# Stationary columns of the feed-forward weights, two or eight elements apart in SBUF

## The chip, the cores and the metric

The kernel runs on one core of a Trainium2 chip. The metric is the time of one execution on the device, in microseconds (us). An execution is timed several times; the median stands for it. One more execution is recorded by the hardware profiler; its page and its trace are what is read below. The engines are named as the profile names them: PE is TensorE (matmuls), PEld its weight loads, DVE VectorE, ACT ScalarE, POOL GpSimd, SP the engine that issues most DMAs.

## The reference

A trunk of two layers works on 256 tokens of 2048 float32 values. Layer 0 is differential attention and a gated feed-forward part with a short causal convolution; layer 1 is a gated DeltaNet and a second such feed-forward part. Each part has a norm before it and is added to the residual stream. The change touches the feed-forward parts alone:

```python
def conv_ffn(h, w_up, conv_w, conv_b, w_down):
    u = causal_dwconv(h @ w_up, conv_w) + conv_b
    val, gate = jnp.split(u, 2, axis=-1)
    return (jax.nn.silu(gate) * val) @ w_down

def reference(x, ...):
    for i in range(DEPTH):
        h = rms_norm(x, mixer_norm[i])
        ...
        x = x + conv_ffn(rms_norm(x, ffn_norm[i]), ffn_w_up[i], ffn_conv_w[i], ffn_conv_b[i], ffn_w_down[i])
    return x
```

The up weights are 2048 x 11008 (5504 values and 5504 gates), the down weights 5504 x 2048, in each layer.

## The kernel before

**Layout.** Activations stand with features on the 128 partitions and the 256 tokens (`T`) along the free dimension; 2048 features are 16 row groups (`KD`), 5504 are 43 (`NJ`). The host lays every weight out in blocks of 256 output columns: `w[block]` has the shape 128 x row groups x 256, where the 256 columns are two column tiles of 128 (`c` = 0 and 1). In an up block, tile 0 holds 128 values and tile 1 the gates that belong to them; in a down block they are neighbours.

**Precision.** A product of float32 is made of three products of a rounded type (`fp32r`): high weight with high activation, low weight with high activation, high weight with low activation. `weights` (lines 81 to 91) loads a chunk of up to four row groups (`CK` = 4, 128 x 1024 elements, 512 KB) into a tile `raw` with one DMA of the SP queue, casts it on ACT into `whi` (line 89) and lets DVE subtract that from `raw` into `wlo` (line 90). Of each of the three there are four buffers, so a chunk's DMA waits until an earlier chunk has been used.

**Products.** `dense` (lines 132 to 156) goes through the chunks of a block. For each row group `k` and column tile `c` it issues two matmuls, here called a pair. Line 151 has a 128x128 piece of `whi` as the stationary operand and 512 moving columns (256 tokens of the high and 256 of the low activation); line 152 has the same piece of `wlo` and 256 moving columns (the high activation). Each matmul is preceded by a load of its stationary operand (LDWEIGHTS in the profile, engine PEld). In the last chunk of a block the two tiles go one after the other, in the others they alternate. `finish` (158 to 167) does the last chunk of the last down block of layer 1, so that each tile's output can be sent off when it is done.

**The order in which columns are read.** Before the change, the stationary operand is `hi[:, k, s]`, 128 elements side by side in each partition. The moving operand goes through `turns` (169 to 171): token `j` of the first 128, token `j` of the second 128, then `j + 1` of each, so that neighbouring reads are 128 elements apart. `halves` (173 to 175) puts the output back in order when it is read from PSUM. The token products `dense_tok` (207 to 224) have the activations as the stationary operand and read the weights as the moving one in the same manner, 256 elements apart.

**The feed-forward part.** `ffn` (364 onwards) runs 43 up blocks, each with 16 row groups. After each block DVE and ACT merge the parts, scale, convolve, and write a gated activation `ac` in its high and low part. Then `project` runs 8 down blocks with 43 row groups each, ten chunks of four and one of three; `add_out` adds them to `x`.

**Order.** The program is straight-line code; each engine runs its instructions in the order in which they are issued, with waits on semaphores for the data of the others. Small work of the attention and DeltaNet parts is spread between the products by generators (`spawn`, `tick`).

Of the kernel before, what the change touches and what calls it, by code (L numbers as in the profile page):

```python
# [16 lines left out]
P = 128  # L17
T = 256
D = 2048
KD = D // P  # L20
EPS = 1e-6
CK = 4
# [4 lines left out]
class Trunk:  # L27
# [101 lines left out]
    def banks(self):  # L129
        return self.dps.tile([P, 2, 2 * T], F32, tag="ps", name="ps")  # L130

    def dense(self, w, kt, acts, tiles=2, wide=True, each=None, apart=False):


        nc = self.nc
        ps = None if each or apart else self.banks()
        bank = [ps[:, c] if ps else self.mp() for c in range(tiles)]
        n = 2 * T if wide else T
        for k0, nk in self.chunks(kt, CK):
            hi, lo = self.weights(w[:, k0:k0 + nk, :])  # L140
            steps = [(k, c) for k in range(nk) for c in range(tiles)]
            if k0 + nk == kt:
                if each:
                    self.finish(bank, hi, lo, k0, nk, acts, each)
                    continue
                steps = [(k, c) for c in range(tiles) for k in range(nk)]
            for k, c in steps:
                a = acts(k0 + k)
                first, last = k0 + k == 0, k0 + k == kt - 1
                s = slice(c * P, (c + 1) * P)  # L150
                nc.tensor.matmul(bank[c][:, :n], hi[:, k, s], self.turns(a[:, :n // T, :]), start=first, stop=False)  # L151
                nc.tensor.matmul(bank[c][:, :T], lo[:, k, s], self.turns(a[:, :1, :]), start=False, stop=last and wide)  # L152
                if not wide:
                    nc.tensor.matmul(bank[c][:, :T], hi[:, k, s], self.turns(a[:, 1:, :]), start=False, stop=last)  # L154
            self.tick()
        return bank if apart else ps

    def finish(self, bank, hi, lo, k0, nk, acts, each):

        nc = self.nc  # L160
        for c in range(2):
            s = slice(c * P, (c + 1) * P)
            for k in range(nk):
                a = self.turns(acts(k0 + k))
                nc.tensor.matmul(bank[c], hi[:, k, s], a, start=False, stop=False)
                nc.tensor.matmul(bank[c][:, :T], lo[:, k, s], self.turns(acts(k0 + k)[:, :1, :]), start=False, stop=k == nk - 1)
            each(c, bank[c].unsqueeze(1))

    def turns(self, a):
# [162 lines left out]
    def pairs(self, a):  # L332

        return a.rearrange("p c t -> p t c") if len(a.shape) == 3 else a.rearrange("p (c t) -> p t c", c=2)
# [15 lines left out]
                done(2 * blk + c)  # L350
            self.add_squares()

    def project(self, w, kt, acts, done, final=False):

        n = KD // 2
        for b in range(n - final):
            self.add_out(b, self.dense(w[b], kt, acts), done)
        if final:
            def each(c, ps):
                self.add_x(KD - 2 + c, 1, ps)  # L360
                done(KD - 2 + c)

            self.dense(w[n - 1], kt, acts, each=each)

    def ffn(self, w_up, w_down, nj, cols_ap, done, final=False):

        nc = self.nc
        self.spawn(self.norm_stat())
        with self.tc.tile_pool(name="fp", bufs=1) as fp:
            cols = fp.tile([P, 8 * nj + 64], F32, tag="fcols", name="fcols")[:, :8 * nj]  # L370
            cols = cols.rearrange("p (t h j) -> p t h j", t=4, h=2)
            nc.scalar.dma_start(cols, cols_ap)
            acts = []
            rows = self.rows(fp.tile([P, nj * 2 * T], F32R, tag="ac", name="ac"), nj)
            for j in range(nj):
                ps = self.dense(w_up[j], KD, self.h_acts)
                c = []
                u = fp.tile([P, 2, T], F32, tag="u", name="u", bufs=2)
                self.merge(ps, u, fp)
                for half in range(2):  # L380
                    o = fp.tile([P, T], F32, tag=f"cv{half}", name="cv", bufs=2)
                    c4 = [cols[:, t, half, j:j + 1] for t in range(4)]
                    self.conv(o, u[:, half, :], c4[:3], c4[3])
                    c.append(o)
                nc.scalar.activation(c[1], c[1], AF.Silu)
                a = c[0]
                nc.vector.tensor_tensor(a, c[0], c[1], ALU.mult)
                ac = rows[j]
                self.split(ac, a)
                acts.append(ac)  # L390
            self.project(w_down, nj, lambda k: acts[k], done, final)

    def attention(self, w_first, w_qk, w_v, w_o, nh, dist_ap, ident_ap, qg, kg, lvec, sub, start, done, lambda_init):

# [531 lines left out]

NH = 8
NJ = 43
NQ = 16
NB, HB = 4, 4  # L930
NV = 2 * NQ

# [6 lines left out]
def _layout(inputs):  # L939
# [3 lines left out]
    x = {k: np.asarray(v) for k, v in inputs.items()}  # L943
# [9 lines left out]
    def blocks(w, kt, starts):  # L953
        w = w.reshape(kt, P, -1)
        return np.stack([np.concatenate([w[:, :, a:a + n] for a, n in s], 2) for s in starts]).transpose(0, 2, 1, 3)

    def pairs(n):
        return [[(T * i, T)] for i in range(n)]

    kd, vd, ff = NQ * P, NV * P, NJ * P  # L960
    wi = x["gdn_w_in"][0]
# [4 lines left out]
    go = x["gdn_w_out"][0].reshape(NB, 2 * HB, P, D // T, T).transpose(0, 3, 2, 1, 4)  # L966
    up = [[(j * P, P), (ff + j * P, P)] for j in range(NJ)]
    q, k = np.arange(P)[:, None], np.arange(T)[None]
# [15 lines left out]
    def turned(w):  # L984
        return w.reshape(*w.shape[:-1], T, 2).swapaxes(-1, -2).reshape(w.shape)

    out = {
        "x": np.concatenate([col[0][:, :KD], x["x"][0].T.reshape(KD, P, T).transpose(1, 0, 2).reshape(P, KD * T)], 1),
        "cols": np.concatenate(col, 1),
# [5 lines left out]
        "dist": np.concatenate(dist, 1),  # L995
        "fcols0": fcols[0],
        "fcols1": fcols[1],
        "w_up0": blocks(x["ffn_w_up"][0], KD, up),
        "w_down0": blocks(x["ffn_w_down"][0], NJ, pairs(D // T)),
        "w_gate": np.pad(wi[:, 2 * kd + 2 * vd:], ((0, 0), (0, P - 2 * NV))).reshape(KD, P, P).transpose(1, 0, 2),  # L1000
        "w_in": blocks(wi, KD, gin),
        "w_z": turned(blocks(wi, KD, gz)),
        "w_out": go.reshape(NB * (D // T), P, 2 * HB, T),
        "gate": np.broadcast_to(np.stack([x["gdn_A_log"][0], x["gdn_dt_bias"][0]]), (P, 2, NV)),
        "const": np.concatenate(const, 1).astype(f),
        "w_up1": blocks(x["ffn_w_up"][1], KD, up),
        "w_down1": blocks(x["ffn_w_down"][1], NJ, pairs(D // T)),
    }
    return {k: np.ascontiguousarray(v) for k, v in out.items()}

# [1 line left out]
def trunk_kernel(tc, a, out):  # L1012
    nc = tc.nc
    with ExitStack() as ctx:
        t = Trunk(ctx, tc)
        n = a["cols"].shape[1]
        cols = t.cp.tile([P, n], F32, tag="cols", name="cols")
        parts = t.chunks(KD, 2)

        def load():  # L1020
            if parts:
                k, n = parts.pop(0)
                s = slice(KD + k * T if k else 0, KD + (k + n) * T)
                nc.sync.dma_start(t.gx[:, s], a["x"][:, s])

        load()
        pos = [0]

        warm = t.mp()
        for _ in range(WARM):  # L1030
            nc.tensor.matmul(warm, t.onesr, t.onesr.unsqueeze(1).to_broadcast([P, 4, P]), start=True, stop=True)

        def take(n):
            pos[0] += n
            return cols[:, pos[0] - n:pos[0]]

        def one(c, i):
            return c[:, i:i + 1]

        mixer, ffn = take(2 * KD), take(2 * KD)  # L1040
        qg, kg, lvec, sub, ng = take(1), take(1), take(4), take(2), take(1)
        gconv = take(4 * 4 * NQ)
        def then(gain, layer):
            return lambda k: t.norm_tile(k, one(gain, layer * KD + k))

        starts = [k for k, _ in parts]
        begun = []

        def start(k):

            if len(begun) <= k:
                if k and k in starts:
                    load()
                if k == KD - 1:
                    with tc.issue_after(t.loaded.ins):
                        nc.sync.dma_start(cols, a["cols"])
                then(t.gx[:, :KD], 0)(k)
                begun.append(k)
            return t.h[k]

        t.attention(a["w_first"], a["w_qk"], a["w_v"], a["w_o"], NH, a["dist"], a["const"][:, :P], qg, kg, lvec, sub, start, then(ffn, 0),
                    0.8 - 0.6 * math.exp(-0.3 * 0))
        t.ffn(a["w_up0"], a["w_down0"], NJ, a["fcols0"], then(mixer, 1))
        t.gdn(a["w_gate"], a["w_in"], a["w_z"], a["w_out"], NB, HB, a["gate"], a["const"],
              lambda tap, tile_: one(gconv, tap * 4 * NQ + tile_), ng, then(ffn, 1))
        t.ffn(a["w_up1"], a["w_down1"], NJ, a["fcols1"],
              lambda k: nc.sync.dma_start(out[:, k, :], t.x[:, k, :]), final=True)


# [13 lines left out]
```

## Time and profile before

| what | value |
|---|---|
| time, median of 3 runs | 2531.76 us (2530.8 to 2531.91) |
| span of the profiled execution | 2530.1 us |
| PE busy | 2520.0 us, 16151 matmuls |
| PEld busy | 2309.7 us, 16151 loads |
| DVE busy | 1908.3 us |
| ACT busy | 1513.2 us |
| HBM read | 482.32 MB, 191 GB/s over the span |

The profiled execution is one of its own; its span goes from the first to the last instruction and is 1.7 us shorter than the median time, which has some launch and end around it. Busy times of different engines overlap, so they don't add up to the span. The duration of a matmul or of a load in a record includes its latency; since matmuls are pipelined, the pace is read from the starts, or from how many there are in a stretch, and not from the durations.

### The profile page before, as it was taken

What the parts mean: (1) busy time and instruction counts of PE and PEld (TensorE: products, weight loads), DVE (VectorE), ACT (ScalarE), POOL (GpSimd) and SP (SyncE); (2) the same over time, 40 slices, a digit from 0 to 9 for tenths busy, and PEclk for the clock granted to TensorE, in tenths of its full rate; (3) what the DMA queues carried; (4) which work ended last, traced back from release to release, by engine and by line L of the source; (5) the groups of instructions that cost most, each with busy time, mean ns of one, the idle gap of its engine ahead of it and who ended that gap; (6) DMA issues with size and microseconds to landing.
All of it is one profiled execution on the core that took longest, in us unless ns stands there. A gap on an engine that the chain in (4) does not pass through costs nothing.

```text
span 2530.1 us, 41598 instructions
## 1 busy us (share of the span) xinstructions
PE 2520.0 (100%) x16151; PEld 2309.7 (91%) x16151; DVE 1908.3 (75%) x2847; ACT 1513.2 (60%) x2098; POOL 103.5 (4%) x197
## 2 busy tenths in 40 slices
PE   9999999999999999999999999999999999999999
PEld 8998899999999999998989989989999999999998
DVE  8886677777777555689788788788887777776544
ACT  7766656666666444485774675675566666665343
POOL 0000000000000000012021021021000000000000
PEclk9999999999999999999999999999999999999999
DMA  7555566666666666666455565555566666666775
GB/s 256 175 184 175 167 203 201 202 202 201 200 201 202 200 200 202 202 187 201 154 185 180 170 188 184 168 175 184 165 201 201 201 201 202 201 201 205 209 207 157
DMA packets 138199, 487.20 MB, mean 193 GB/s; under 512 B 15472, under 2 KB 18448, under 8 KB 138000
## 3 DMA queue, kind: packets, MB, share of 16 engines
q1 hardware_dynamic: 137712, 484.17, 60.8%
q8 instruction: 127, 2.08, 0.3%
q14 instruction: 72, 0.59, 0.1%
q10 hardware_dynamic: 288, 0.35, 0.0%
HBM read 482.32 MB, written 2.15 MB: 191 GB/s over the span
## 4 chain that ended last, share of the span: by engine, by line
PE 95%; ACT 3%; DVE 1%; issue 1%; DMA 0%; SPq 0%; ACTq 0%; DVEq 0%
PE ps L151 51%; PE ps L152 26%; PE ps L221 3%; PE ps L220 3%; PE ps L222 3%; PE mp L773 2%; PE mp L151 1%; PE ps L154 1%; ACT whi L89 1%; PE mp L329 1%; PE mp L152 0%; ACT L593 0%; ACT lt L631 0%; PE ps L123 0%; ACT L297 0%
## 5 line engine op out<-in xcount | busy, mean ns | idle before, releaser
L90 DVE TENSOR_TENSOR wlo<-raw,whi 128x1024 fp32r<-128x1024 f32 (+2 forms) x911 | 1104.1, 1213 | 506.1 <-ACT whi L89 498.2
L89 ACT CAST whi<-raw 128x1024 fp32r<-128x1024 f32 (+2 forms) x911 | 944.2, 1038 | 822.9 <-PE ps L151 657.0
L151 PE MATMUL ps<-h,whi 128*128 128x512 f32 (+1 forms) x4208 | 1369.4, 375 | 0.0
L152 PE MATMUL ps<-h,wlo 128*128 128x256 f32 x4208 | 1151.1, 274 | 1.0 <-DVE wlo L90 1.0
L151 PEld LDWEIGHTS ps<-h,whi 128*128 128x128 f32 x4208 | 796.1, 189 | 102.8
L152 PEld LDWEIGHTS ps<-h,wlo 128*128 128x128 f32 x4208 | 807.7, 192 | 2.8 <-DVE wlo L90 1.3
L151 PE MATMUL ps<-ac,whi 128*128 128x512 f32 x1546 | 506.8, 382 | 0.0
L152 PE MATMUL ps<-ac,wlo 128*128 128x256 f32 x1546 | 421.2, 273 | 0.0
L151 PEld LDWEIGHTS ps<-ac,whi 128*128 128x128 f32 x1546 | 292.1, 189 | 40.8 <-PE ps L151 0.2
L152 PEld LDWEIGHTS ps<-ac,wlo 128*128 128x128 f32 x1546 | 296.8, 192 | 0.1
L151 PE MATMUL ps<-oc,whi 128*128 128x512 f32 x512 | 170.7, 384 | 0.0
L220 PE MATMUL ps<-whi,h 128*128 128x512 f32 x384 | 146.5, 382 | 0.0
L221 PE MATMUL ps<-wlo,h 128*128 128x512 f32 x384 | 146.1, 380 | 0.0
L222 PE MATMUL ps<-whi,h 128*128 128x512 f32 x384 | 145.7, 379 | 0.0
L310 DVE SCALAR_TENSOR_TENSOR cv<-u,fcols,cv 128x255 f32<-128x255 f32 (+1 forms) x344 | 142.9, 477 | 0.0
L152 PE MATMUL ps<-oc,wlo 128*128 128x256 f32 x512 | 142.0, 277 | 0.0
L151 PEld LDWEIGHTS ps<-oc,whi 128*128 128x128 f32 x512 | 96.9, 189 | 12.5
L152 PEld LDWEIGHTS ps<-oc,wlo 128*128 128x128 f32 x512 | 98.3, 192 | 0.5
L308 ACT ACTIVATE cv<-u,fcols 128x256 f32<-128x256 f32 x172 | 93.9, 593 | 0.5 <-DVE u L205 0.5
L343 DVE TENSOR_TENSOR x<-ps,x 128x512 f32<-128x512 f32 x110 | 75.6, 687 | 12.5 <-PE ps L152 11.2
L310 DVE SCALAR_TENSOR_TENSOR cv<-u,cols,cv 128x255 f32<-128x255 f32 (+2 forms) x192 | 84.0, 486 | 0.3
L221 PEld LDWEIGHTS ps<-wlo,h 128*128 128x128 f32 x384 | 72.6, 189 | 10.0 <-DVE wlo L90 0.2
(220 smaller groups left out, 2077.3 us busy)
## 6 DMA issues: line engine op xcount, KB each, us to landing
raw<-w_up SPq DMA_DIRECT2D x344, 512.0 KB, 4.7
raw<-w_down SPq DMA_DIRECT2D x160, 512.0 KB, 3.8
raw<-w_in SPq DMA_DIRECT2D x128, 512.0 KB, 4.7
raw<-w_z SPq DMA_DIRECT2D x64, 512.0 KB, 3.7
raw<-w_out SPq DMA_DIRECT2D x64, 512.0 KB, 4.2
raw<-w_qk SPq DMA_DIRECT2D x56, 512.0 KB, 4.5
raw<-w_v SPq DMA_DIRECT2D x32, 512.0 KB, 3.5
raw<-w_o SPq DMA_DIRECT2D x32, 512.0 KB, 4.7
```

What stands on the lines that cost most here:

```text
L89: self.cast = nc.scalar.copy(hi[:, :, s], raw[:, :, s])
L90: nc.vector.tensor_tensor(lo[:, :, s], raw[:, :, s], hi[:, :, s].bitcast(F32), ALU.subtract)
L151: nc.tensor.matmul(bank[c][:, :n], hi[:, k, s], self.turns(a[:, :n // T, :]), start=first, stop=False)
L152: nc.tensor.matmul(bank[c][:, :T], lo[:, k, s], self.turns(a[:, :1, :]), start=False, stop=last and wide)
L154: nc.tensor.matmul(bank[c][:, :T], hi[:, k, s], self.turns(a[:, 1:, :]), start=False, stop=last)
L220: nc.tensor.matmul(ps[:, c, :], ah, wh, start=first, stop=False)
L221: nc.tensor.matmul(ps[:, c, :], ah, wl, start=False, stop=False)
L222: nc.tensor.matmul(ps[:, c, :], al, wh, start=False, stop=last)
L308: nc.scalar.activation(out, u, AF.Identity, bias=bias, scale=taps[n - 1])
L310: nc.vector.scalar_tensor_tensor(out[:, j:], u[:, :T - j], taps[n - 1 - j], out[:, j:], ALU.mult, ALU.add)
L343: self.nc.vector.tensor_tensor(x, part, x, ALU.add)
L773: nc.tensor.matmul(p[:, v, :], l(v), r[:, v, :], start=i == 0, stop=i == len(terms) - 1)
```

## The change

Only the feed-forward weights are touched. A function `column` takes the stationary piece for row group `k` and column tile `c` out of a tile in one of three ways: side by side as before, `"column"`, or `"chunk"`. In the way `"column"` the two column tiles of a row group are interleaved, so that neighbouring columns of one tile lie two elements apart. In the way `"chunk"` the row groups of the chunk and the two column tiles are all interleaved, so that neighbouring columns lie eight elements apart (six in a chunk of three row groups). The host writes the weights in that order (`ways` in `_layout`); which stationary piece is multiplied with what stays the same. Layer 0 has `"column"` in its up products and `"chunk"` in its down products, layer 1 the other way round. All other products keep the old layout.

```diff
+    def column(self, w, k, c, way):
+
+        nk = w.shape[1]
+        if way == "column":
+            return w[:, k].rearrange("p (j c) -> p c j", c=2)[:, c]
+        if way == "chunk":
+            return w.rearrange("p k n -> p (k n)").rearrange("p (j k c) -> p k c j", k=nk, c=2)[:, k, c]
+        return w[:, k, c * P:(c + 1) * P]
+
-    def dense(self, w, kt, acts, tiles=2, wide=True, each=None, apart=False):
-
+    def dense(self, w, kt, acts, tiles=2, wide=True, each=None, apart=False, way=None):
...
-                s = slice(c * P, (c + 1) * P)
-                nc.tensor.matmul(bank[c][:, :n], hi[:, k, s], self.turns(a[:, :n // T, :]), start=first, stop=False)
-                nc.tensor.matmul(bank[c][:, :T], lo[:, k, s], self.turns(a[:, :1, :]), start=False, stop=last and wide)
+                wh, wl = self.column(hi, k, c, way), self.column(lo, k, c, way)
+                nc.tensor.matmul(bank[c][:, :n], wh, self.turns(a[:, :n // T, :]), start=first, stop=False)
+                nc.tensor.matmul(bank[c][:, :T], wl, self.turns(a[:, :1, :]), start=False, stop=last and wide)
...
-                ps = self.dense(w_up[j], KD, self.h_acts)
+                ps = self.dense(w_up[j], KD, self.h_acts, way=ways[0])
...
-            self.project(w_down, nj, lambda k: acts[k], done, final)
+            self.project(w_down, nj, lambda k: acts[k], done, final, ways[1])
...
+WAYS = ("column", "chunk"), ("chunk", "column")
...
+    def ways(w, way):
+        if way == "column":
+            return w.reshape(*w.shape[:-1], 2, P).swapaxes(-1, -2).reshape(w.shape)
+        r = np.empty_like(w)
+        for k in range(0, w.shape[2], CK):
+            v = w[:, :, k:k + CK]
+            r[:, :, k:k + CK] = np.moveaxis(v.reshape(*v.shape[:-1], 2, P), -1, 2).reshape(v.shape)
+        return r
...
-        "w_up0": blocks(x["ffn_w_up"][0], KD, up),
-        "w_down0": blocks(x["ffn_w_down"][0], NJ, pairs(D // T)),
+        "w_up0": ways(blocks(x["ffn_w_up"][0], KD, up), WAYS[0][0]),
+        "w_down0": ways(blocks(x["ffn_w_down"][0], NJ, pairs(D // T)), WAYS[0][1]),
```

`finish` has the same edit as `dense`, `w_up1` and `w_down1` the same as `w_up0` and `w_down0` with `WAYS[1]`, and the two calls of `ffn` pass `ways=WAYS[0]` and `ways=WAYS[1]`.

More of the change, by code (lines that the diff above doesn't have):

```diff
@@ L143, in dense @@
                 if each:
-                    self.finish(bank, hi, lo, k0, nk, acts, each)
+                    self.finish(bank, hi, lo, k0, nk, acts, each, way)
                     continue
@@ L149, in dense, with finish @@
                 first, last = k0 + k == 0, k0 + k == kt - 1
-                s = slice(c * P, (c + 1) * P)
-                nc.tensor.matmul(bank[c][:, :n], hi[:, k, s], self.turns(a[:, :n // T, :]), start=first, stop=False)
-                nc.tensor.matmul(bank[c][:, :T], lo[:, k, s], self.turns(a[:, :1, :]), start=False, stop=last and wide)
+                wh, wl = self.column(hi, k, c, way), self.column(lo, k, c, way)
+                nc.tensor.matmul(bank[c][:, :n], wh, self.turns(a[:, :n // T, :]), start=first, stop=False)
+                nc.tensor.matmul(bank[c][:, :T], wl, self.turns(a[:, :1, :]), start=False, stop=last and wide)
                 if not wide:
-                    nc.tensor.matmul(bank[c][:, :T], hi[:, k, s], self.turns(a[:, 1:, :]), start=False, stop=last)
+                    nc.tensor.matmul(bank[c][:, :T], wh, self.turns(a[:, 1:, :]), start=False, stop=last)
             self.tick()
         return bank if apart else ps
-    def finish(self, bank, hi, lo, k0, nk, acts, each):
+    def finish(self, bank, hi, lo, k0, nk, acts, each, way):
         nc = self.nc
         for c in range(2):
-            s = slice(c * P, (c + 1) * P)
             for k in range(nk):
                 a = self.turns(acts(k0 + k))
-                nc.tensor.matmul(bank[c], hi[:, k, s], a, start=False, stop=False)
-                nc.tensor.matmul(bank[c][:, :T], lo[:, k, s], self.turns(acts(k0 + k)[:, :1, :]), start=False, stop=k == nk - 1)
+                wh, wl = self.column(hi, k, c, way), self.column(lo, k, c, way)
+                nc.tensor.matmul(bank[c], wh, a, start=False, stop=False)
+                nc.tensor.matmul(bank[c][:, :T], wl, self.turns(acts(k0 + k)[:, :1, :]), start=False, stop=k == nk - 1)
             each(c, bank[c].unsqueeze(1))
@@ L351, in add_out, with project @@
             self.add_squares()
-    def project(self, w, kt, acts, done, final=False):
+    def project(self, w, kt, acts, done, final=False, way=None):
         n = KD // 2
         for b in range(n - final):
-            self.add_out(b, self.dense(w[b], kt, acts), done)
+            self.add_out(b, self.dense(w[b], kt, acts, way=way), done)
         if final:
@@ L361, in each, with ffn @@
                 done(KD - 2 + c)
-            self.dense(w[n - 1], kt, acts, each=each)
-    def ffn(self, w_up, w_down, nj, cols_ap, done, final=False):
+            self.dense(w[n - 1], kt, acts, each=each, way=way)
+    def ffn(self, w_up, w_down, nj, cols_ap, done, final=False, ways=(None, None)):
         nc = self.nc
@@ L1005, in _layout @@
         "const": np.concatenate(const, 1).astype(f),
-        "w_up1": blocks(x["ffn_w_up"][1], KD, up),
-        "w_down1": blocks(x["ffn_w_down"][1], NJ, pairs(D // T)),
+        "w_up1": ways(blocks(x["ffn_w_up"][1], KD, up), WAYS[1][0]),
+        "w_down1": ways(blocks(x["ffn_w_down"][1], NJ, pairs(D // T)), WAYS[1][1]),
     }
@@ L1062, in trunk_kernel @@
                     0.8 - 0.6 * math.exp(-0.3 * 0))
-        t.ffn(a["w_up0"], a["w_down0"], NJ, a["fcols0"], then(mixer, 1))
+        t.ffn(a["w_up0"], a["w_down0"], NJ, a["fcols0"], then(mixer, 1), ways=WAYS[0])
         t.gdn(a["w_gate"], a["w_in"], a["w_z"], a["w_out"], NB, HB, a["gate"], a["const"],
@@ L1066, in trunk_kernel @@
         t.ffn(a["w_up1"], a["w_down1"], NJ, a["fcols1"],
-              lambda k: nc.sync.dma_start(out[:, k, :], t.x[:, k, :]), final=True)
+              lambda k: nc.sync.dma_start(out[:, k, :], t.x[:, k, :]), final=True, ways=WAYS[1])
 def kernel(**inputs):
```

## Prediction

> **What bounds the kernel now.** First the head of the page: the span, the busy shares, the granted clock, and the chain that ended last.
>
> ```profile
> span 2530.1 us, 41598 instructions
> PE 2520.0 (100%) x16151; PEld 2309.7 (91%) x16151; DVE 1908.3 (75%) x2847; ACT 1513.2 (60%) x2098; POOL 103.5 (4%) x197
> ...
> PEclk9999999999999999999999999999999999999999
> ...
> PE 95%; ACT 3%; DVE 1%; issue 1%; DMA 0%; SPq 0%; ACTq 0%; DVEq 0%
> ```
>
> TensorE is the bound: its matmuls cover the span, the chain of work that ended last lies on it for 95%, and the clock is whole throughout. A busy share says nothing yet about whether the matmuls themselves or the weight loads between them set the pace. So the next view is that of busy time by stretch, in the four stages that the change touches (up and down products of layer 0, then of layer 1).
>
> ```profile
> 500.00:600.00 100.00, 100.00 (x612) 91.93 (x611) 78.82 (x114) 61.67 (x87) 0.00 (x0) 1.00 0.62 201
> 880.00:980.00 100.00, 100.00 (x613) 91.92 (x612) 58.03 (x64) 45.84 (x55) 0.00 (x0) 1.00 0.69 201
> 1900.00:2000.00 100.00, 100.00 (x613) 91.92 (x612) 78.83 (x113) 61.53 (x86) 0.00 (x0) 1.00 0.61 201
> 2340.00:2440.00 100.00, 100.00 (x612) 92.07 (x612) 50.32 (x45) 39.77 (x40) 0.00 (x0) 1.00 0.71 208
> 1852.00:2300.00 448.00, 448.00 (x2739) 411.95 (x2738) 357.21 (x517) 279.68 (x389) 0.00 (x0) 1.00 0.62 201
> ```
>
> The columns are PE, PEld, DVE, ACT, POOL, then the clock, the DMA share and GB/s. All four stages run at one pace: 448.00 us for 2739 matmuls is 163.6 ns each, 327.1 ns for a pair of one 512-column matmul with a high part and one 256-column matmul with a low part. Nothing else is late there: DVE is at most 79% busy and the DMA engines 71%. What happens inside a pair is in the timeline.
>
> ```profile
> 700.12 0.27 PE L152 MATMUL ps<-h,wlo 128*128 128x256 f32 x1
> 700.13 0.19 PEld L151 LDWEIGHTS ps<-h,whi 128*128 128x128 f32 x1
> 700.23 0.38 PE L151 MATMUL ps<-h,whi 128*128 128x512 f32 x1
> 700.24 0.19 PEld L152 LDWEIGHTS ps<-h,wlo 128*128 128x128 f32 x1
> 700.45 0.27 PE L152 MATMUL ps<-h,wlo 128*128 128x256 f32 x1
> ```
>
> Each load starts just behind the start of a matmul and must be through before the next matmul. The load of a low part has the 0.22 us of a 512-column matmul to hide in, the load of a high part only the 0.11 us of a 256-column one. How long does the reading of the columns take? Records of loads of 32, 64 and 128 columns tell it apart from their fixed part.
>
> ```profile
> L151 PEld LDWEIGHTS ps<-h,whi 128*128 128x128 f32 x4208 | 796.1, 189 | 102.8
> L152 PEld LDWEIGHTS ps<-ac,wlo 128*128 128x128 f32 x1546 | 296.8, 192 | 0.1
> L738 PEld LDWEIGHTS mp<-TT,Ta 64*64 64x64 f32 x128 | 8.0, 134 | 1.8 <-issue 1.8
> L724 PEld LDWEIGHTS mp<-ttc,pc 32*32 32x32 f32 x256 | 4.4, 108 | 0.9 <-issue 0.5 <-ACT u L582 0.2 <-ACT whi L89 0.2
> ```
>
> From 32 to 128 columns the record grows by 81 ns (108 to 189), 0.84 ns a column, so 128 columns take about 108 ns and the rest of a record is latency. That is as long as the slot of a 256-column matmul. Two other stages show which of the two ends the slot.
>
> ```profile
> 1079.83 0.28 PE L152 MATMUL ps<-h,wlo 128*128 128x256 f32 x1
> ...
> 1080.95 0.28 PE L154 MATMUL ps<-h,whi 128*128 128x256 f32 x1
> ```
>
> ```profile
> 1243.93 0.82 PE L818 MATMUL mp<-con,zt 128*128 128x128 f32 x6
> 1244.58 0.39 PE L773 MATMUL mp<-vt,TT 128*128 128x128 f32 x2
> ```
>
> ```profile
> L818 PEld LDWEIGHTS mp<-con,zt x64: 138/141/146, 1242.6 to 1804.2; 128*128 128x128 f32 x64
> ```
>
> In the first, eleven 256-column matmuls in a row stand between those starts (ten steps), each with a load of its own: 1.12 us / 10 = 112 ns. In the second, six transposes take 0.65 us, 108 ns each, with loads of 141 ns, some 50 ns shorter. So a slot with a short load costs 108 ns, and one with a load of the long kind 112 ns. **The load of a high part is already what ends its slot, by some 4 ns; it has no cover left.** That is the fact on which everything below rests.
>
> **The change part by part.** The host lays each feed-forward weight out anew, with the same bytes in runs of the same length: the DMAs, the casts to the high part and the subtractions still see whole 128x1024 tiles in address order. I cost these three at nothing, and no queue is reordered. Their cover is wide in any case: the casts wait for TensorE, not the other way round.
>
> ```profile
> ACT whi L89 <- PE ps L151: 657.0, 532, 2.9
> raw<-w_up SPq DMA_DIRECT2D x344, 512.0 KB, 4.7
> raw<-w_down SPq DMA_DIRECT2D x160, 512.0 KB, 3.8
> ```
>
> The first row is of the view of waits: ACT waits 657 us in all until matmuls give a buffer free. The waits and semaphores of the program are not touched, as each cast still writes a whole tile and each matmul still waits for that tile. Instructions are neither added nor removed.
>
> What is left is the address order in which loads read their 128 columns. In the code, an up product has 43 blocks x 16 row groups x 2 column tiles = 1376 pairs, a down product 8 x 43 x 2 = 688. At 327.1 ns a pair, the 4128 pairs of both layers are 1350 us, 53% of the span. Steps of eight elements (32 bytes; six in the last chunk of a down product, which has three row groups) fall on the down product of layer 0 and the up product of layer 1, 688 + 1376 = 2064 pairs; steps of two (8 bytes) on the other 2064.
>
> No row of before shows a load with a step, so I bound it. *Upper end.* The nearest row in which an engine reads and writes float32 with long steps is a transpose of VectorE (line 682: steps of 16 elements read, 32 written), beside one of the same size without steps (line 684).
>
> ```profile
> L682 DVE STREAM_TRANSPOSE tcc<-Ti x4: 1123/1136/1159, 1189.7 to 1727.9; 128x512 f32<-128x512 f32 x4
> L684 DVE STREAM_TRANSPOSE ttc<-tcc x4: 690/694/698, 1191.3 to 1729.4; 128x512 f32<-128x512 f32 x4
> ```
>
> The difference, 1136 - 694 = 442 ns over 512 elements, is 0.86 ns an element for two stepped sides, at most 110 ns for a load of 128 columns, if all of it were on the read side. Paid by the steps of eight only: a high load then takes 218 ns, its slot grows by 110 ns, and the slot of the low load, now 218 + 4 ns against 215 (327.1 - 112), grows by 7: 2064 x 117 ns = 241 us. With half of it for the read side, 55 ns, low loads stay hidden (163 ns in 215), and the cost is 2064 x 55 ns = 114 us. *Lower end.* A shorter load can give back only the 4 ns that it now costs its slot: 4128 x 4 ns = 17 us at most, if both steps did it.
>
> *What I take.* The nearest row is not VectorE's but that of the other operand of the same matmuls. By the code (`turns`), moving columns are read alternately from two places 128 elements apart, 256 elements in the token products, so that no two reads in a row fall together:
>
> ```profile
> 231.69 0.38 PE L220 MATMUL ps<-whi,h 128*128 128x512 f32 x1
> ...
> 232.99 0.38 PE L220 MATMUL ps<-whi,h 128*128 128x512 f32 x1
> ```
>
> Six steps of such 512-column matmuls take 1.30 us, 217 ns each, 0.42 ns a column. TensorE takes in moving float32 columns from steps far longer than eight elements at twice the pace at which it reads stationary columns. If the path of the loads is of the same make, 0.84 ns a column leaves room for a new place with every column. So I take zero for both steps, and keep 17 us below and 241 us above. [...]
>
> [...]
>
> The sum: 2530.1 us of span + 0 = 2530.1 us. The median of the runs, 2531.76 us, lies 1.7 us above the profiled span, the time around it. **Forecast 2531.8 us.**
>
> **The rivals.** *Slower: a step of eight makes the load longer.* It has one place, the 2064 slots of 256 columns, and decides from the first ns, as those slots have no cover: above 2.5 ns a load (5.1 us / 2064) it is measurable. By half of line 682's price it gives 2531.8 + 114 = 2646 us, by all of it 2531.8 + 241 = 2773 us. For it: zero cover, and the stepped transposes. Against it: the moving operand. *Faster: a step lets the load run ahead.* If columns in a row now hinder each other, apart from one another they load faster, and the slots fall from 112 towards 108 ns: 2531.8 - 17 = 2515 us if both steps do it, 2523 if one does. For it: moving columns that are read from two places in turn run at the full pace. Against it: no row shows contiguous moving columns of this type at full clock, so the trace has no sign that closeness hurts; and the short loads of the transposes are contiguous by the code. *Nothing is changed for the chip:* steps are merged away before they reach TensorE. That gives 2531.8 as well, with the contiguous weights of the host then read wrongly; the diff gives no sign of it.
>
> **How the numbers follow.** Forecast 0.50, with 0.02 more for no change on the chip; faster 0.13; slower 0.35, of which 0.07 between 2537 and 2600, 0.16 about 2646, 0.12 from 2650 up to 2773 and beyond (steps of two paying too). A measurement can tell some 0.2%, 5 us. So faster 0.13, same 0.52, slower 0.35. The forecast's own range is 2527 to 2537. For 8 in 10 the range must reach into the slow case: 2515 to 2650 leaves out 0.12 above and a few hundredths below.
>
> **What would show it.** Right: the four windows still hold about 612 matmuls in 100 us, loads stay at 189 and 192 ns, pairs at 327 ns. The slow rival: the windows of the down product of layer 0 and the up product of layer 1 hold fewer, about 524 (pairs of 382 ns) or 450 (444 ns), and the records of their high loads grow by 55 to 110 ns, while the other two stages stay as they are. The fast rival: 614 to 620 matmuls in the windows. [...]

## The result, and the profile after

The changed kernel takes 2862.23 us (median of 4 runs, 2862.07 to 2862.52) against 2531.78 us before (4 runs): 1.131 times as long, 95% interval 1.129 to 1.132, or 330.5 us more. That is outside the predicted range, and even beyond the 2773 us of the dearest case with a price.

The page of the changed kernel, its head and the chain that ended last:

```profile
span 2860.7 us, 41598 instructions
PE 2851.1 (100%) x16151; PEld 2709.3 (95%) x16151; DVE 1914.0 (67%) x2847; ACT 1504.7 (53%) x2098; POOL 103.1 (4%) x197
...
PEclk9999999999999999999999999999999999999999
...
PE 95%; ACT 3%; issue 1%; DVE 1%; DMA 0%; SPq 0%; ACTq 0%; DVEq 0%
```

The instructions are as many as before, the clock is whole, DVE and ACT work within 1% as long as before, and TensorE covers the span again. So nothing waits for a new partner; TensorE's own work has become longer. The view of busy time by stretch shows where, in the same order of stages as in the prediction (columns: PE, PEld, DVE, ACT, POOL, clock, DMA share, GB/s):

```profile
500.00:600.00 100.00, 100.00 (x601) 94.25 (x601) 79.12 (x115) 60.24 (x86) 0.00 (x0) 1.00 0.62 197
950.00:1050.00 100.00, 100.00 (x417) 100.00 (x417) 40.93 (x45) 32.51 (x39) 0.00 (x0) 1.00 0.47 139
2200.00:2300.00 100.00, 100.00 (x416) 100.00 (x416) 55.03 (x79) 40.86 (x60) 0.00 (x0) 1.00 0.44 136
2700.00:2800.00 100.00, 100.00 (x603) 93.80 (x602) 49.73 (x46) 39.17 (x39) 0.00 (x0) 1.00 0.70 207
```

The two middle rows are the stages with steps of eight elements: 416 or 417 matmuls in 100 us instead of 612, so 481 ns a pair instead of 327. There the records of the weight loads (PEld) cover 100% of the stretch, against 92% before. That alone doesn't show that the loads set the pace, as PE is covered as well; the experiments below do. The outer rows are the stages with steps of two: 601 to 603 matmuls, 333 ns a pair. The DMA share falls in the middle rows because chunks are used up more slowly: from 2200 to 2300 us the casts wait 48.4 us for matmuls to free a buffer, and the view of waits lists no wait for a DMA there.

The groups of loads in the stage with steps of eight (2200 to 2300 us; the mean of one in ns stands behind the busy time) and in that with steps of two (500 to 600 us):

```profile
L160 PEld LDWEIGHTS ps<-h,wlo 128*128 128x128 f32 x208 | 70.5, 339 | 0.0
L159 PEld LDWEIGHTS ps<-h,whi 128*128 128x128 f32 x208 | 70.4, 338 | 0.0
```

```profile
L160 PEld LDWEIGHTS ps<-h,wlo 128*128 128x128 f32 x301 | 59.4, 198 | 0.0
L159 PEld LDWEIGHTS ps<-h,whi 128*128 128x128 f32 x300 | 58.5, 195 | 5.8
```

A load's record grew from 189 to 338 ns with steps of eight, and to 195 ns with steps of two. From the first 512-column matmul of a stage to its last, a pair takes 480.9 instead of 327.5 ns in the down product of layer 0, 483.2 instead of 328.1 in the up product of layer 1, and 5.8 or 5.9 ns more than before in the two stages with steps of two. So 688 x 153.4 ns + 1376 x 155.1 ns + 2064 x 5.9 ns = 106 + 213 + 12 = 331 us, and the spans differ by 330.6 us. The whole loss is in the pairs of these four stages.

### The profile page after: what moved, and what is told of

Same layout as the page of the kernel before. It is cut to its first block, busy times and chain, and to the rows that moved or that the text cites. A ratio compares the mean times of both kernels' runs of the same rounds, so it can differ in the third digit from the quotient of the medians.

```text
span 2860.7 us, 41598 instructions
## 1 busy us (share of the span) xinstructions
PE 2851.1 (100%) x16151; PEld 2709.3 (95%) x16151; DVE 1914.0 (67%) x2847; ACT 1504.7 (53%) x2098; POOL 103.1 (4%) x197
## 4 chain that ended last, share of the span: by engine, by line
PE 95%; ACT 3%; issue 1%; DVE 1%; DMA 0%; SPq 0%; ACTq 0%; DVEq 0%
PE ps L159 54%; PE ps L160 25%; PE ps L229 3%; PE ps L228 3%; PE ps L230 3%; PE mp L781 1%; PE mp L159 1%; ACT whi L89 1%; PE ps L162 1%; PE mp L337 1%; ACT L601 0%; PE mp L160 0%; ACT lt L639 0%; PE ps L123 0%; ACT L305 0%
## 5 line engine op out<-in xcount | busy, mean ns | idle before, releaser
L159 PE MATMUL ps<-h,whi 128*128 128x512 f32 (+1 forms) x4208 | 1590.6, 419 | 0.0
L160 PE MATMUL ps<-h,wlo 128*128 128x256 f32 x4208 | 1187.4, 282 | 0.8 <-DVE wlo L90 0.8
L159 PEld LDWEIGHTS ps<-h,whi 128*128 128x128 f32 x4208 | 1010.0, 240 | 56.6
L160 PEld LDWEIGHTS ps<-h,wlo 128*128 128x128 f32 x4208 | 1017.7, 242 | 2.6 <-DVE wlo L90 1.1
L159 PE MATMUL ps<-ac,whi 128*128 128x512 f32 x1546 | 615.8, 441 | 0.0
L160 PE MATMUL ps<-ac,wlo 128*128 128x256 f32 x1546 | 438.6, 284 | 0.0
L159 PEld LDWEIGHTS ps<-ac,whi 128*128 128x128 f32 x1546 | 397.7, 257 | 19.3 <-PE ps L159 0.2
L160 PEld LDWEIGHTS ps<-ac,wlo 128*128 128x128 f32 x1546 | 399.5, 258 | 0.1
```

Source lines behind the costliest of these rows:

```text
L159: nc.tensor.matmul(bank[c][:, :n], wh, self.turns(a[:, :n // T, :]), start=first, stop=False)
L160: nc.tensor.matmul(bank[c][:, :T], wl, self.turns(a[:, :1, :]), start=False, stop=last and wide)
```

## The experiments

### Each kind of step alone

Two kernels keep one kind of step and undo the other.

```diff
-WAYS = ("column", "chunk"), ("chunk", "column")
+WAYS = ("column", "column"), ("column", "column")
```

> Steps of two elements in all four products, none of eight. If the two steps act independently and each slot of 256 columns pays by its own load: 4128 pairs x 5.9 ns = 24 us, 2556 us, load records 195 to 198 ns, pairs of 333 ns in all four stages. If steps of two are free by themselves and only paid beside steps of eight: 2532 us.

```diff
-WAYS = ("column", "chunk"), ("chunk", "column")
+WAYS = (None, "chunk"), ("chunk", None)
...
     def ways(w, way):
+        if way is None:
+            return w
```

> Steps of eight in the down products of layer 0 and the up products of layer 1, all others contiguous as before. Independent: 2064 pairs x 153.7 ns = 317 us, 2849 us, and 327 ns a pair in the contiguous stages. If a stage is also slowed by what its neighbour does: the contiguous stages lie above 327 ns.

Measured: 2555.92 us with steps of two everywhere (ratio 1.009, interval 1.008 to 1.011; the kernel before, timed beside it, took 2532.22), all four stages at 601 or 602 matmuls in 100 us; and 2850.53 us with steps of eight in their two stages alone (ratio 1.126, interval 1.124 to 1.128). The windows of the latter, same stages as above:

```profile
500.00:600.00 100.00, 100.00 (x612) 91.95 (x611) 78.84 (x114) 61.27 (x85) 0.00 (x0) 1.00 0.59 201
950.00:1050.00 100.00, 100.00 (x418) 100.00 (x418) 41.09 (x45) 31.98 (x39) 0.00 (x0) 1.00 0.44 138
2200.00:2300.00 100.00, 100.00 (x417) 100.00 (x416) 54.40 (x77) 41.29 (x59) 0.00 (x0) 1.00 0.42 137
2650.00:2750.00 100.00, 100.00 (x613) 91.92 (x612) 50.58 (x45) 39.98 (x40) 0.00 (x0) 1.00 0.68 210
```

The contiguous stages are back at 612, the others stay. The parts add up: 318.3 us for the steps of eight, half of 23.7 us for two stages with steps of two, together 330.2 of the 330.5 us. No stage slows its neighbour.

### One load of a pair alone

```diff
-                wh, wl = self.column(hi, k, c, way), self.column(lo, k, c, way)
+                wh, wl = self.column(hi, k, c, way and way[0]), self.column(lo, k, c, way and way[1])
...
-WAYS = ("column", "chunk"), ("chunk", "column")
+WAYS = (("column", None), (None, "column")), (("chunk", None), (None, "chunk"))
...
     def ways(w, way):
+        return w
```

> The weights lie in the old order, and only one of the two loads of a pair reads with a step (the pieces multiplied are then other columns than the reference's): high loads by two in the up products of layer 0, low loads by two in the down products of layer 0, high loads by eight in the up products of layer 1, low loads by eight in the down products of layer 1. Theory of the slots (a load costs only what exceeds the streaming of the matmul before it: 112 ns behind 256 columns, 215 behind 512): pairs of 333, 327, 455 and 352 ns, 2733 us in all. Rival (each stepped load costs the same wherever it stands, half of the loss of its pair): 330, 330, 404 and 404 ns, 2697 us.

Measured: 2728.23 us in one run, near the 2733 of the theory of the slots and not the 2697 of its rival. The windows, in the order high by two, low by two, high by eight, low by eight:

```profile
500.00:600.00 100.00, 100.00 (x602) 92.00 (x602) 78.12 (x115) 60.77 (x85) 0.00 (x0) 1.00 0.58 198
900.00:1000.00 100.00, 100.00 (x612) 94.11 (x611) 54.59 (x57) 44.22 (x51) 0.00 (x0) 1.00 0.66 204
2200.00:2300.00 100.00, 100.00 (x443) 94.08 (x442) 58.42 (x83) 42.83 (x62) 0.00 (x0) 1.00 0.44 144
2550.00:2650.00 100.00, 100.00 (x573) 100.00 (x571) 46.91 (x42) 37.95 (x37) 0.00 (x0) 1.00 0.63 193
```

From the starts, pairs take 333, 327, 453 and 350 ns, against 333, 327, 455 and 352 by the theory of the slots and 330, 330, 404, 404 by its rival. So a load costs what exceeds the streaming of the matmul beside it. The same step of two is free where the load has 512 columns to hide in, and paid where it has 256. A load by eight costs its 256-column slot 126 ns (453 - 327) and its 512-column slot 23 ns. This part of the prediction, the zero cover of the high load, holds.

### How long a load takes by its step, with little else going on

What makes the stepped load long? This kernel is the one before with groups of 32 matmuls behind the last product:

```diff
+        def many(name, w, a, n):
+            out = self.mps.tile([P, 512], F32, tag="mp", name=name)
+            for _ in range(32):
+                self.nc.tensor.matmul(out[:, :n], w, a, start=True, stop=True)
...
+        def step(s, n):
+            return hs[:, :n * s].rearrange("p (j s) -> p s j", s=s)[:, 0]
+
+        def places(q, d, n):
+            return hs[:, :q * d].rearrange("p (q d) -> p d q", q=q)[:, :n // q]
...
+        for s in (1, 2, 3, 4, 5, 6, 7, 8, 12, 16, 32, 64):
+            many(f"st{s}", step(s, P) if s > 1 else hs[:, :P], a, T)
+        many("odd1", hs[:, 2:P + 2], a, T)
+        many("wide8", step(8, P), self.turns(self.h[0]), 2 * T)
+        many("small1", hs[:, :P], hs[:, :32], 32)
+        many("small8", step(8, P), hs[:, :32], 32)
+        w = hs[:, :P]
+        many("m1", w, hs[:, :512], 512)
+        for s in (2, 4, 8, 16):
+            many(f"m{s}", w, step(s, 512), 512)
+        many("mturn", w, self.turns(self.h[0]), 512)
+        for q in (2, 4, 8, 32):
+            many(f"mq{q}", w, places(q, T, 512), 512)
```

> The kernel before, and behind its last product 23 groups of 32 matmuls each, on the activations h, whose results nobody reads. Each group has its own step between the stationary columns (256 moving columns unless said otherwise) or its own order of the moving columns (contiguous stationary). DVE, ACT and the DMA queues have little or nothing to do in this stretch. Theory A (pieces of 16 bytes, four elements): a load takes about 1.84 ns for each such piece that it opens (235 ns / 128 columns in the changed kernel), and not less than 0.84 ns a column; start to start 112 ns at step 1, 118 at step 2 (64 pieces), some 180 at step 3 (96 pieces), 240 at 4, 5, 6, 7, 8, 12, 16, 32 and 64; the record of a load at step 8 about 338 ns. Theory B (length of the step): 3 to 7 rise evenly from 118 to 240, and 16, 32 and 64 lie above 240. Theory C (other traffic in SBUF disturbs the stepped loads): step 8 here is close to 112 ns, since the casts, the subtractions and the DMAs are gone. Step 8 with 512 moving columns: 240 by A and B, 216 by C. Step 8 with 32 moving columns: 240 by A; less if it were the moving reads that disturb it. Moving columns: contiguous and from two places in turn 216 ns for 512. Theory D (places that are returned to stay open): steps of 4, 8 and 16 elements, which never return, are slower than 216, and some number of places read in turn is too many. Rival to D (the moving reads don't care): 216 for every order.

Each window below reaches from the first start of one group to the first start of the next, so that its length divided by 32 is the pace (the counts hold up to three more, still running at an edge). Stationary steps of 1, 2, 4, 8 and 16:

```profile
2525.97:2529.54 3.57, 3.57 (x34) 3.57 (x33) 0.95 (x3) 0.00 (x0) 0.00 (x0) 1.00 0.22 73
2529.54:2533.38 3.84, 3.84 (x35) 3.84 (x33) 0.00 (x0) 0.00 (x0) 0.00 (x0) 1.00 0.00 0
2539.08:2546.55 7.47, 7.47 (x34) 7.47 (x33) 0.00 (x0) 0.00 (x0) 0.00 (x0) 1.00 0.00 0
2568.43:2576.11 7.68, 7.68 (x34) 7.68 (x33) 0.00 (x0) 0.00 (x0) 0.00 (x0) 1.00 0.00 0
2584.64:2591.76 7.12, 7.12 (x33) 7.12 (x33) 0.00 (x0) 0.00 (x0) 0.00 (x0) 1.00 0.00 0
```

3.57 us / 32 = 112 ns at step 1, 120 at 2, 233 at 4, 240 at 8. All medians of the distances between starts:

| step of the stationary columns | 1 | 2 | 3 | 4 | 5 | 6 | 7 | 8 | 12 | 16, 32, 64 |
|---|---|---|---|---|---|---|---|---|---|---|
| ns a load | 112 | 120 | 178 | 233 | 227 | 227 | 231 | 240 | 267 | 220 |

Theory C falls: in the window of step 8, DVE, ACT and the DMA engines do nothing, and the load takes 240 ns, as in the kernel. With 32 moving columns instead of 256 it still takes 238 ns, and with 512 it takes 242, so the moving reads are not to blame either. Theory B falls, since steps of 16 to 64 are cheaper than one of 8. Theory A comes close: 178 (180 expected), 233 and 240 (240), with 220 and 267 as its worst misses. From step 2 on, a load takes 1.7 to 2.1 ns for each piece of four elements in which its columns lie: 120 ns for 64 pieces (step 2), 178 for 96 (step 3), and 220 to 267 for the 128 pieces of steps of 4 and more, about twice as long as the 112 ns of contiguous columns. That is a fit to these times; the trace doesn't show how a load reads.

The group with contiguous loads and only 32 moving columns bears on the fact on which the prediction rests:

```profile
2617.23:2620.72 3.49, 3.49 (x33) 3.49 (x32) 0.00 (x0) 0.00 (x0) 0.00 (x0) 1.00 0.02 5
```

Its starts are 112 ns apart (the median; only the first distance, 28 ns, is shorter than 111), the same as with 256 columns. So the load alone fills the slot beside 256 columns, and whatever lengthens it lengthens the slot.

The moving side, 512 columns each: steps of 2, 4 and 16, two places in turn, then four and eight places in turn.

```profile
2637.66:2652.14 14.48, 14.48 (x34) 6.62 (x32) 0.00 (x0) 0.00 (x0) 0.00 (x0) 1.00 0.00 0
...
2652.14:2666.90 14.76, 14.76 (x34) 6.67 (x32) 0.00 (x0) 0.00 (x0) 0.00 (x0) 1.00 0.01 1
2680.70:2694.56 13.86, 13.86 (x33) 6.59 (x32) 0.00 (x0) 0.00 (x0) 0.00 (x0) 1.00 0.00 0
2694.56:2701.49 6.93, 6.93 (x34) 6.06 (x32) 0.00 (x0) 0.00 (x0) 0.00 (x0) 1.00 0.00 0
2708.39:2717.44 9.05, 9.05 (x33) 6.14 (x32) 0.00 (x0) 0.00 (x0) 0.00 (x0) 1.00 0.00 0
2717.44:2733.01 15.57, 15.57 (x33) 6.67 (x32) 0.00 (x0) 0.00 (x0) 0.00 (x0) 1.00 0.00 0
```

14.48 us / 32 = 452 ns at step 2, 461 at 4, 433 at 16; 217 (median 216) with two places in turn; 283 with four and 487 with eight. The times are those of theory D: moving columns are not free to lie anywhere. Two places in turn run at the pace of the kernel before (216 ns, there 217). Returns alone are not enough, as reads from four or eight places in turn return too. With steps of 4, 8 and 16, which never return to a place, columns take twice as long, 0.84 to 0.90 ns each; a step of 2 is no better (0.88). (The contiguous group of this run fell in a stretch with a granted clock of 0.82 on average, from 2630 to 2637 us, and is measured again below.)

### Does a step add as much to the load of a transpose?

A moving column from a place of its own costs 0.84 to 0.90 ns, a stationary one some 1.7 to 1.9, and 2.1 at step 12. Does the second price hold for every load, some 1.8 ns for each piece of four elements (theory L below)? The loads of transposes, whose 140 ns records are the short kind, can tell.

```diff
+        for s, name in ((1, "ta"), (2, "tb"), (4, "td"), (8, "th"), (16, "tp")):
+            out = group(name)
+            for _ in range(32):
+                self.nc.tensor.transpose(out[:, :P], step(x, s, P), ident)
+        many("fa", x[:, :P], x[:, :P], P)
+        many("fh", step(x, 8, P), x[:, :P], P)
+        w = hs[:, :P]
+        many("ma", w, hs[:, :512], 512)
+        many("nd", w, near(4), 512)
+        many("nh", w, near(8), 512)
+        many("nx", w, near(64), 512)
+        many("md", w, step(hs, 4, 512), 512)
```

> The kernel before, and behind its last product 12 groups of 32 instructions whose results nobody reads: transposes of a float32 tile, with steps of 1, 2, 4, 8 and 16 elements between the stationary columns; plain float32 products of 128 moving columns with stationary steps of 1 and 8; and products of 512 moving columns, contiguous, from two places in turn that are 4, 8 and 64 elements apart, and with a step of 4. [...] Theory L (1.8 ns for each place that is opened, whoever reads): 200 at step 2, 310 to 330 at 4 and 8, 300 at 16. [...] Moving columns: 226 ns contiguous at full clock, 461 at step 4; two places in turn 216 at every distance if two open places are what counts, or near 226 at distances of 4 and 8 if they have to lie far apart.

The groups of loads in that stretch, by tile: transposes at steps 1, 4, 8 and 16 (`ta`, `td`, `th`, `tp`), plain float32 products at step 8 (`fh`), which hold two matmuls each:

```profile
L180 PEld LDWEIGHTS fh<-x 128*128 128x128 f32 x64 | 15.3, 335 | 0.0
...
L191 PEld LDWEIGHTS td<-eye,x 128*128 128x128 f32 x32 | 3.9, 209 | 0.0
...
L191 PEld LDWEIGHTS th<-eye,x 128*128 128x128 f32 x32 | 3.7, 193 | 0.0
L191 PEld LDWEIGHTS tp<-eye,x 128*128 128x128 f32 x32 | 3.7, 193 | 0.0
L191 PEld LDWEIGHTS ta<-eye,x 128*128 128x128 f32 x32 | 3.5, 140 | 0.0
```

Transposes come out at 140, 209 (steps 2 and 4), and 193 ns (8 and 16), far from theory L (310 to 330 at 4 and 8, 300 at 16). A step of eight adds 53 ns to the load of a transpose and 149 ns to that of a product; a step of two adds 69 and 6 ns. Plain float32 products take 112 and 238 ns a load at steps 1 and 8, like the others. So the price of a step depends on the kind of load; why, the runs don't show.

Contiguous moving columns take 227 ns at a granted clock of 1.00, two places in turn 216 whether 4, 8 or 64 elements apart, and a step of 4 takes 461 again.

### The moving side in the kernel

If contiguous moving columns are the slower ones, then the order that the prediction leaned on must itself be worth something. This kernel is the one before without it:

```diff
-        return a.rearrange("p i (q j) -> p i j q", q=2)
+        return a.rearrange("p i (q j) -> p i q j", q=2)
...
-        return [ps[:, :, i * T:(i + 1) * T].rearrange("p c (j q) -> p c q j", q=2) for i in range(2)]
+        return [ps[:, :, i * T:(i + 1) * T].rearrange("p c (q j) -> p c q j", q=2) for i in range(2)]
...
-        return w.reshape(*w.shape[:-1], T, 2).swapaxes(-1, -2).reshape(w.shape)
+        return w
```

> The kernel before with contiguous stationary and also contiguous moving columns: turns, halves and the layout of w_z and w_v leave the order of the tokens and columns as it is. If the reading rule holds for the moving side in the kernel as in the separate measurement (226.6 instead of 215.8 ns for 512 columns, 115.6 instead of 112 for 256): 7328 x 10.7 ns + 6992 x 3.6 ns = 104 us, 2636 us, pairs of 342 ns. Rival (the moving order is free in the kernel, and the separate measurement was disturbed by its half clock): 2532 us.

Measured: 2700.85 us, ratio 1.067 (1.065 to 1.069).

```profile
500.00:600.00 100.00, 100.00 (x568) 86.83 (x567) 75.31 (x107) 56.76 (x81) 0.00 (x0) 1.00 0.57 187
```

The rival (2532 us) falls. The sign is right, the size was 65 us short: pairs take 353 ns (100 us / 567 x 2), not 342. A last run of groups asked whether the other engines add the rest, and mapped more steps:

```diff
+        pairs("pa", w, v, a, b)
+        pairs("pb", w, v, hs[:, :T], hs[:, :512])
+        pairs("pc", hs[:, :P], hs[:, :P], hs[:, :T], hs[:, :512])
+        for s, name in ((8, "qa"), (9, "qb"), (10, "qc"), (12, "qd"), (14, "qe"), (16, "qf"), (20, "qg"), (24, "qh"), (48, "qi")):
+            many(name, step(hs, s, P), a, T)
```

> The kernel before, and behind its last product 12 groups whose results nobody reads: 32 pairs of 512 and 256 moving columns, from two places in turn, and contiguous with the stationary pieces far from or among the moving columns; and 32 products each of 256 moving columns with stationary steps of 8, 9, 10, 12, 14, 16, 20, 24 and 48 elements. Pairs: 327 ns in turn; contiguous 342 ns (226.6 + 115.6) if nothing else disturbs them here and the 353 ns of the kernel come from the other engines' traffic, 353 ns if the pair by itself is that slow. Steps: 240 at 8 and 267 at 12 again. If it is places of 64 bytes that tell (a step of 16 or more always leaves them), 9, 10 and 14 lie between 220 and 270 and everything from 16 up is 220; if it is multiples of four elements, 9, 10 and 14 are about 220 to 230, and 20, 24 and 48 lie above 220 as well.

The 32 pairs in turn, then contiguous with the stationary pieces far from the moving columns, then among them:

```profile
2526.04:2536.52 10.48, 10.48 (x67) 9.65 (x65) 0.95 (x3) 0.00 (x0) 0.00 (x0) 1.00 0.08 25
2536.52:2547.82 11.30, 11.30 (x66) 9.80 (x65) 0.00 (x0) 0.00 (x0) 0.00 (x0) 1.00 0.01 1
2547.82:2559.13 11.31, 11.31 (x66) 9.80 (x65) 0.00 (x0) 0.00 (x0) 0.00 (x0) 1.00 0.00 0
```

A pair takes 327 ns in turn (10.48 us / 32) and 353 ns contiguous (11.30 us / 32), with the other engines at rest and wherever the stationary pieces lie. So a contiguous pair is as slow by itself as in the kernel; adding up groups of one length (226.6 + 115.6) was the wrong sum. Steps of 8, 9, 10, 12, 14, 16, 20, 24 and 48 take 240, 240, 231, 267, 244, 220, 236, 251 and 220 ns. Neither guess fits: 9, 10 and 14 match the 64-byte one, 20 and 24 don't. What makes 12 dearer than 16 (by 47 ns), and 8, 9, 14, 20 and 24 (by 16 to 31 ns), stays open; against the doubling from 112 it is a small part of the cost, and not the cause of the result.

## Why the prediction was wrong

**What held.** TensorE stays the bound, no wait is added, the DMAs and casts keep their cover, and the loss lies only in the loads. The load of a high part had no cover: in the one-load kernel the smallest lengthening, 6 ns, appears in full there and not at all behind 512 columns, and a contiguous load sets a slot of 112 ns even beside 32 columns. The two rows from which the prediction drew this did not show it by themselves: its 108 ns slots are transposes of 128 moving columns and its 112 ns slots are products of 256, so more than the load differs between them. The conclusion was right, the proof came later. The signs set out for the slow rival came in kind, but not in size: the windows of its two stages held 416 or 417 matmuls instead of 524 or 450, and the low loads grew as much as the high ones. The other two stages, which were to stay as they are, fell from 612 to between 601 and 603. The premise of the fast rival, that neighbouring columns hinder each other, holds for moving columns (227 ns contiguous, 216 in turn), but no step made a load shorter than 112 ns.

**The step that failed is the choice of the nearest row.** The prediction took the moving operand, read 128 or 256 elements apart at 0.42 ns a column, as a sign that TensorE can change its place with every column, and so put the steps of eight at zero; they cost 318 us. But those reads return to the same two places, and steps of eight return to none. The first measurement shows that this was the matter: moving columns with a step of 4, which don't come back, take 461 ns, not 216. Even returns help only while the places are few, as eight places in turn take 487. So the moving order was no witness for steps of eight.

**The second error is the size of the bound.** The upper end came from a VectorE transpose, 110 ns a load. The record grew by 149 ns and the slots by 126 + 23 ns when taken singly, 154 together, against 117 in the sum. With 110 ns for all of it, 2773 us was the dearest case worked out; 2862 us lay outside. A row of another engine is no bound on this one. Nor would the right moving row have been enough: at 0.84 to 0.90 ns a column, 128 columns are at most 115 ns, and the loads took 240. That 0.84 ns a column leaves room for a new place with every column was the author's estimate, and the loads showed no such room: at steps of 4 and more they took 1.7 to 2.1 ns a column.

**Steps of two** were put at zero and cost 6 ns a high load, 12 us of the 330 here and 24 us when used throughout, clear of noise.

## What to carry to other kernels

Where a 128-column float32 load runs beside a matmul of 256 columns, the load already ends the slot (112 ns beside 256 columns and beside 32), so the stationary columns should stay contiguous: four elements apart or more, a load took 220 to 267 ns instead of 112 with the other engines at rest, and by eight as long in the kernel too (481 ns for a pair, with two loads). A stride that is free on one operand proves nothing for another (moving columns from two places in turn took 216 ns for 512, as fast as any order measured); ask whether the reads return to their places, and measure a group of 32 with that very pattern behind the kernel. A layout that must have a step can have a small one on the loads that stand beside 512 columns: steps of two there cost nothing (327 ns a pair, as before).

No version tried beats the kernel before; its contiguous stationary columns were the fastest of all steps measured.

## What the runs showed of the hardware

- Two places in turn beat contiguous moving columns of this type: 216 against 227 ns for 512 columns in groups, 327 against 353 ns in pairs, and 2531 against 2701 us for the kernel. Two places only 4 elements apart took 216 ns as well.
- Four places in turn cost 283 ns, eight 487, thirty-two 553, so in these groups returns to a place helped only while the places were few.
- The pace of a stepped load did not follow the clock granted to TensorE. The group with a step of eight and 32 moving columns, at a granted clock of 0.60 on average, took 7.63 us / 32 = 238 ns a load, against 240 at 1.00. The contiguous moving columns just behind it did follow: from 2628.35 to 2637.66 us, 291 ns for 512, with a clock of 0.82 in the part from 2630 to 2637 us, and 227 at 1.00.

```profile
2620.72:2628.35 7.63, 7.63 (x34) 7.63 (x34) 0.00 (x0) 0.00 (x0) 0.00 (x0) 0.60 0.00 0
2630.00:2637.00 7.00, 7.00 (x27) 5.63 (x27) 0.00 (x0) 0.00 (x0) 0.00 (x0) 0.82 0.00 0
```
